# Strassen's algorithm for most of the input projection in an encoder-layer kernel

## The chip, the cores and the metric

The kernel runs on one core of a Trainium2 chip. The metric is the device time of one launch in microseconds (us): the median of three runs before the change is 1462.85 us (1462.04 to 1463.18). Engines are named as the profile names them: PE (matrix products; PEld is its weight load), DVE (vector), ACT (activation), POOL (GpSimd), SP (its queue issues the transfers, here called DMAs).

## The reference

One layer over 1024 tokens of width 1024. What the change touches is the first half:

```python
h = rmsnorm(x, g_mix_pre); proj = h @ w_in          # q, k, v of 8 + 8 heads of 64, and 8 forget gates
f_logit = proj[gates] + b_fgt; c = cumsum(log_sigmoid(f_logit))
y_fox = softmax(q k^T / 8 + c_t - c_s, causal) v    # 8 "f" heads
y_chk = softmax(q k^T / 8 + bias(t - s), band) v    # 8 "c" heads: own chunk of 64 + 8 before
y = concat(rmsnorm(y_fox), rmsnorm(y_chk)); x = x + rmsnorm(y @ w_out)
# then cross-attention into 256 memory tokens (mem), then a squared-ReLU MLP
```

## The kernel before

All products run in full float32 accuracy by splitting each operand in a high part (rounded to the engine's fp32r) and a low remainder, and doing three products (high-high, high-low, low-high): `mm3`, lines 193 to 195. A 128x128 block of weights times 512 tokens is therefore three PE instructions. 

Tokens are held transposed and split in `hT[th]`, th = 0, 1 for the two halves of 512 tokens. Heads come in eight pairs (`ORDER`, line 359: c0, c1, f0 to f3, c2, c3). A pair's queries are one block of 128 columns of `w_in`, its keys another, and for pairs 4 to 7 its values a third; the values of pairs 0 to 3 and the forget gates are made ahead. `project_steps` makes one such block: for each half of the tokens 8 blocks of contraction, so 2 x 8 x 3 = 48 PE instructions of 128x512. ACT and DVE take the result out of the accumulator in halves of 64 partitions (one head each): queries as scaled high and low parts stacked in one tile (`qs`), keys as a high tile `kd` and a low tile `kl`, each of which a DMA then copies to the other 64 partitions (line 849).

The order of everything is planned when the kernel is built. `Flow` is a list scheduler with guessed durations: streams of PE steps are generators (`value_steps`, `turn_steps`, `score_steps`, `side_steps`, `rstd_steps`, `filler_steps`), tried in that order, and whatever is ready first is issued; work of V (DVE), S (ACT), G (POOL) and D (the SP queue) is put in queues with levels. `Tokens` count free buffers (`u4`: tiles of 4 KB in each partition, 30 in all; `klo`, `sp`, `raw`, `w`, `mm` and so on). The chip then runs this fixed order on each engine, with semaphores for what the plan only guessed. The filler is the projection of all pairs and then the memory keys (`mk`) and values (`mv`); attention comes first wherever it can.

Attention of a head is a score product, a softmax (DVE, ACT, POOL), a transpose of the probabilities on the PE (line 711), their split (lines 717, 720) and the product with the values (line 754). The accumulator then holds four blocks, for the probabilities' high and low parts and the values' high and low parts on the two halves of the partitions. They are added in three steps: ACT copies one half of the partitions (771), DVE adds the other (766), POOL adds the high and low columns (768), and SP stores 64 rows in `od` (761).

The gates are turned to 8 rows of 1024 and put through eight vector operations there (`forget_gates`). The memory rows are normalised with their gain, stored in DRAM and loaded again (`mem_norm`, `mem_loads`).

Later parts of the kernel (the MLP and the first half of the memory output projection) already use Strassen's algorithm; the change does not touch them.

Of the kernel before, what the change touches and what calls it, by code (L numbers as in the profile page):

```python
# [22 lines left out]
P = 128  # L23
S = 1024
# [31 lines left out]
class Flow:  # L56
# [17 lines left out]

    def load(self, at, call, then=None, took=4.5, level=0):
        self.put("D", at, 0.55, call, then and (lambda end: then(end + took)), level)

    def chain(self, at, parts, then=None, level=2):

        if not parts:  # L80
            return then and then(at)
        eng, cost, call = parts[0]
        more = lambda end: self.chain(end + (2.5 if eng == "D" else 0.05), parts[1:], then, level)
        self.put(eng, at, cost, call, more, level)
# [21 lines left out]
    def run(self, streams, more=lambda: False):  # L106
        heads = [[g, next(g, None)] for g in streams]
        idle = 0
        while any(h[1] for h in heads) or more():
            for pump in self.pumps:  # L110
                pump()
            for h in heads:
                if h[1] and h[1][1]():
                    cost = h[1][0]
                    self.end = self.now + cost + 0.2
                    h[1] = next(h[0], None)
                    self.upto(self.now + cost)
                    idle = 0
                    break
            else:  # L120
                idle += 1
                assert idle < 4000, "no step can be taken"
                self.upto(self.now + 0.05)
# [12 lines left out]
def build(ctx, tc, nc, out, t):  # L136
# [106 lines left out]
    bfgt = const.tile([8, 1], F32, name="bfgt")  # L243
    gcol = const.tile([P, KC], F32, name="gcol")

    od = [[dr.tile([P, HT], F32, name=f"od{k}_{h}") for h in range(2)] for k in range(KC)]
    x1d = [dr.tile([P, D], F32, name=f"x1d{b}") for b in range(TB)]
    x2d = [dr.tile([P, D], F32, name=f"x2d{b}") for b in range(TB)]
    rd = dr.tile([8, 768], F32, name="rd")
    md = [dr.tile([P, D], F32, name=f"md{b}") for b in range(2)]  # L250
    cd = dr.tile([8, S], F32, name="cd")
    td = {k: [dr.tile([P, 2, HT], F32, name=f"{k}d{i}") for i in range(2)] for k in ("T1", "T2", "T3", "T4")}
# [23 lines left out]
    def bias_rows(part):  # L276

        if part == 0:
            rows.extend(p1.tile([8, 768], F32, tag="sp", bufs=5, name=k) for k in ("rrow", "rsrc"))
# [8 lines left out]
    fcol = p1.tile([P, TB, 8], F32, tag="o2", bufs=2, name="fcol")  # L288
# [52 lines left out]
    def value_leave(g, kb, ps):  # L341
# [12 lines left out]
        if g == 0:  # L354
# [9 lines left out]
                 q=4, mp=4, pt=1, xt=2, wq=0).items()}  # L364
    seen = {}

# [3 lines left out]
    def mark(key):  # L370
        return lambda at: seen.__setitem__(key, at)

# [12 lines left out]

    class Stock:
# [3 lines left out]
        def __init__(self):  # L390
            self.blocks = []
            for n, (kind, pr) in enumerate(ORDER):
                if n == 5:
                    self.blocks.append("norm")
                b = (0 if kind == "f" else 8) + pr
                self.blocks.append((("q", n), t["w_qk"][b], [P, KC, P]))
                if n > 3:
                    self.blocks.append((("v", n), t["w_v"][n - 4], [P, KC, P]))
                if n == 7:
                    self.blocks.append("mem")  # L400
                self.blocks.append((("k", n), t["w_qk"][b + 4], [P, KC, P]))
# [25 lines left out]
            self.raw, self.w, self.turned = {}, {}, 0  # L427
            self.to_load, self.to_split = list(self.blocks), []

        def load(self, n=1):  # L430
            for _ in range(n):
# [4 lines left out]
                self.to_split.append(key)  # L436
# [23 lines left out]
        def split_now(self, n):  # L460
# [6 lines left out]
            seen.update({("raw", key): 0.0 for key in self.to_split})  # L467
# [6 lines left out]
        def pump(self):  # L474

            while self.to_load:
                if isinstance(self.to_load[0], str):
                    n = 3 if self.to_load[0] == "norm" else 2
                    if not free["raw"].ready(n):
                        break  # L480
                    for _ in range(n):
                        free["raw"].take()
                    (mem_norm if self.to_load.pop(0) == "norm" else mem_loads)()
                    break
# [6 lines left out]
            while self.to_split and there(("raw", self.to_split[0])):  # L491
                key = self.to_split[0]
                home = self.home.get(key, "w")
# [19 lines left out]

    def forget_gates():

        z, e, l, u = [p1.tile([8, S], F32, tag="sp", bufs=5, name=f"f{n}") for n in "zelu"]
        parts = []
        for g in range(2):
            tr = mm_tile([8, 4, P], f"ftr{g}", "tr")
            for j in range(4):  # L520
                nc.tensor.transpose(tr[:, j, :], fcol[:, g * 4 + j, :], ident)
            parts.append(("V", 0.75, lambda g=g, tr=tr: nc.vector.tensor_scalar(
                z[:, g * HT:(g + 1) * HT], tr.rearrange("p a b -> p (a b)"), bfgt, None, op0=ALU.add)))

        parts += [
            ("V", 0.7, lambda: nc.vector.tensor_scalar(l, z, -1.0, None, op0=ALU.mult)),
            ("V", 1.2, lambda: nc.vector.tensor_tensor(l, l, z, op=ALU.min)),
            ("S", 1.1, lambda: nc.scalar.activation(e, l, AF.Exp)),
            ("V", 0.7, lambda: nc.vector.tensor_scalar(u, e, 1.0, None, op0=ALU.add)),
            ("S", 2.4, lambda: nc.scalar.activation(l, u, AF.Ln)),  # L530
            ("V", 1.3, lambda: nc.vector.scalar_tensor_tensor(e, u, 1.0, e, op0=ALU.subtract, op1=ALU.subtract)),
            ("S", 2.4, lambda: nc.scalar.activation(u, l, AF.Exp, scale=-1.0)),
            ("V", 1.2, lambda: nc.vector.tensor_tensor(e, e, u, op=ALU.mult)),
            ("V", 1.2, lambda: nc.vector.tensor_sub(e, e, l)),
            ("V", 1.3, lambda: nc.vector.scalar_tensor_tensor(e, z, 0.0, e, op0=ALU.min, op1=ALU.add)),
            ("V", 0.9, lambda: nc.vector.memset(u, 0.0)),
            ("V", 2.3, lambda: nc.vector.tensor_tensor_scan(l, e, u, 0.0, op0=ALU.add, op1=ALU.add)),
            ("D", 0.55, lambda: nc.sync.dma_start(cd, l))]

        def done(at):  # L540
            seen["gates"] = at
            for _ in range(4):
                free["sp"].give(at)

        for _ in range(2):
            free["tr"].take()
        flow.chain(flow.end, parts[:2], lambda at: [free["tr"].give(at) for _ in range(2)] and
                   flow.chain(at, parts[2:], done))
# [55 lines left out]
    def score_steps():  # L604
# [5 lines left out]
        for n, a in heads:  # L610
            kind, pr = ORDER[n]
            h = pr * 2 + a
            for g in groups(n):
                probs[n, a, g] = {}
                for q in (1, 0) if kind == "f" else (0, 1):
# [9 lines left out]
                    for j, (o, w) in enumerate(pieces):  # L625
# [3 lines left out]
                               lambda: there(("qk", n), ("bias", n, a)) and free["s"].ready()  # L629
# [96 lines left out]
    def value_steps():  # L726
        landed = [all_of(("od", k), 32) for k in range(2)]
        for n, a, g in units:
            kind, pr = ORDER[n]
            h = pr * 2 + a  # L730
            own, oth = HALVES[a]
# [25 lines left out]
            def leave(pv=pv, kind=kind, nm=f"{n}{a}{g}", own=own, oth=oth, kcol=kcol, g=g, step=1 if kind == "f" else -1):  # L757
                o2 = p1.tile([P, 2, 2, P], F32, tag="o2", bufs=2, name=f"o2{nm}")

                def store(end):  # L760
                    flow.load(end, lambda: nc.sync.dma_start(
                        od[kcol][g // 2][own, (g % 2) * 256:(g % 2) * 256 + 256],
                        o2[own, 0].rearrange("p a b -> p (a b)")), landed["fc".index(kind)], 2.2)

                def both(at):
                    flow.put("V", at, 0.7, lambda: nc.vector.tensor_add(  # L766
                        o2[own], pv[own, :, :, ::step], o2[own]), lambda end: (
                        free["pv"].give(end), flow.put("G", end, 0.8, lambda: nc.gpsimd.tensor_add(  # L768
                            o2[own, 0], o2[own, 0], o2[own, 1]), store)))

                flow.put("S", flow.end, 0.6, lambda: nc.scalar.activation(o2[own], pv[oth, :, :, ::step], AF.Copy), both)  # L771
# [20 lines left out]
    def project_steps(what, n, part):  # L792
# [6 lines left out]
        u = 3 if what == "v" else 2  # L799
        for th in range(2):  # L800
            cs = slice(th * HT, (th + 1) * HT)
            for kc in range(KC):
                yield (0.681, lambda: kc or there((what, n)) and free["mm"].ready() and
                       (th or free["u4"].ready(u) and (what != "k" or free["klo"].ready(2))))
                if kc == 0:
                    free["mm"].take()
                    if th == 0:
                        for _ in range(u):
                            free["u4"].take()
                        if what == "k":  # L810
                            for _ in range(2):
                                free["klo"].take()
# [3 lines left out]
            if what == "v":  # L816
                if th == 0:
                    vt[n] = u4(f"vt{n}", (P, S), F32)
                    vs2[n] = [u4(f"vs2_{n}{i}", (P, 4, 2, P)) for i in range(2)]
                flow.put("S", flow.end, 0.6, lambda th=th, ps=ps, cs=cs: nc.scalar.activation(vt[n][:, cs], ps, AF.Copy),  # L820
                         lambda at, th=th: (free["mm"].give(at), seen.__setitem__(("vt", n, th), at)), 1)
                continue
# [8 lines left out]
            for a, (own, oth) in enumerate(HALVES):  # L831
# [5 lines left out]
                if what == "q":  # L837
# [5 lines left out]
                    flow.put("S", flow.end, 0.6, hi, lambda at, lo=lo, last=last: flow.put(  # L843
                        "V", at, 0.7, lo, lambda end: (last(end), part(end)), 1), 1)
                else:
# [5 lines left out]
                    def then(at, lo=lo, last=last, copy=copy, d=d, l=l):  # L851
                        flow.load(at, lambda: copy(d), part, 2.3)
# [1614 lines left out]
```

## Time and profile before

| what | value |
|---|---|
| median of three runs | 1462.85 us |
| span of the profiled execution, first to last instruction | 1459.5 us |
| PE / DVE / ACT / POOL busy in it | 1447.7 / 996.0 / 820.7 / 421.0 us |
| instructions on PE | 7265 |
| bytes moved by DMA | 232.17 MB, 159 GB/s on average |
| first projection block (q of pair 0) starts | 56.8 us |
| last memory value product starts | 515.2 us |

The span is that of the one profiled execution; what lies between it and the launch's time is not in the profile. "Busy" of the PE counts overlapping instructions, so 99% says little of how dense its work is: the distance from one matmul's start to the next does. In the views by windows, the columns are the busy time of each engine with the number of instructions, the granted PE clock, the mean busy share of the 16 DMA engines, and GB/s.

### The profile page before, as it was taken

The page shows a single profiled execution, that of the slowest core. Times are in us where ns is not written, and L with a number is a line of the kernel's source. Part 1 is how long each engine was busy: PE and PEld are TensorE (multiplying, and loading weights), DVE is VectorE, ACT ScalarE, POOL GpSimd, SP SyncE. Part 2 cuts the span into 40 slices and gives each one's busy share as a digit, 9 for nine tenths or more (in the row PEclk, how much of TensorE's full clock was granted, in tenths as well). Part 3 has the DMA queues.
Part 4 walks back from the last instruction along what each step waited for, and adds up shares of the span by engine and source line. Part 5 has one row for each costly group of instructions (what it writes and reads, how often), then busy time and mean ns, then how long its engine had stood idle before and what let it go on. Part 6 is the DMA issues. An engine that isn't in the chain of part 4 may idle for free.

```text
span 1459.5 us, 21037 instructions
## 1 busy us (share of the span) xinstructions
PE 1447.7 (99%) x7265; PEld 1222.2 (84%) x7265; DVE 996.0 (68%) x1704; ACT 820.7 (56%) x1437; POOL 421.0 (29%) x520
## 2 busy tenths in 40 slices
PE   9999999999999999999999999999999999999998
PEld 8988888888889888888788888888888888888886
DVE  6777777767668847976873687765555666655576
ACT  6567677766677836555653465545555543444442
POOL 1245456555455301521332414343322000000021
PEclk9999999999999999999999999999999999999999
DMA  7132324321325584552541637754444785445565
GB/s 276 49 95 72 83 67 140 86 82 46 95 58 161 174 314 173 187 179 86 181 138 44 200 132 260 258 196 159 159 151 161 286 318 185 140 149 190 186 246 202
DMA packets 88987, 232.17 MB, mean 159 GB/s; under 512 B 10649, under 2 KB 14753, under 8 KB 88881
## 3 DMA queue, kind: packets, MB, share of 16 engines
q1 hardware_dynamic: 88736, 230.57, 47.6%
q8 instruction: 57, 0.93, 0.3%
q14 instruction: 50, 0.40, 0.1%
q10 hardware_dynamic: 144, 0.26, 0.1%
HBM read 167.30 MB, written 55.11 MB: 152 GB/s over the span
## 4 chain that ended last, share of the span: by engine, by line
PE 96%; DVE 2%; DMA 1%; ACT 1%; issue 0%; SPq 0%; DVEq 0%; ACTq 0%
PE pv L754 4%; PE fx L194 4%; PE fx L193 4%; PE fx L195 4%; PE ptr L711 4%; PE px L194 3%; PE fy L193 3%; PE px L195 3%; PE fy L195 3%; PE px L193 3%; PE fy L194 3%; PE mq L195 2%; PE q L193 2%; PE q L195 2%; PE q L194 2%; PE yw L193 2%
## 5 line engine op out<-in xcount | busy, mean ns | idle before, releaser
L717 DVE TENSOR_TENSOR phl<-ptr,phl 128x512 fp32r<-128x512 f32 (+1 forms) x152 | 92.5, 616 | 31.5 <-ACT phl L720 30.5
L2163 ACT ACTIVATE whif<-ra 128x1024 fp32r<-128x1024 f32 x37 | 39.2, 1061 | 130.3 <-PE fy L194 62.6
L2165 DVE TENSOR_TENSOR wlof<-ra,whif 128x1024 fp32r<-128x1024 f32 x37 | 45.3, 1225 | 91.7 <-ACT whif L2163 91.7
L720 ACT ACTIVATE phl<-ptr 128x512 fp32r<-128x512 f32 (+1 forms) x152 | 79.8, 540 | 40.3 <-PE ptr L711 38.5
L2285 POOL TENSOR_SCALAR rf<-sf 128x1 f32<-128x1 f32 x7 | 7.9, 1130 | 321.7 <-ACT jf L2266 321.4
L754 PE MATMUL pv<-phl,vs 128*128 128x512 f32 (+1 forms) x304 | 85.2, 366 | 0.2 <-DVE phl L717 0.2
L193 PE MATMUL fx<-vhif,whif 128*128 128x512 f32 x168 | 65.4, 389 | 0.0
L195 PE MATMUL fx<-vhif,wlof 128*128 128x512 f32 x168 | 65.4, 389 | 0.0
L194 PE MATMUL fx<-vlof,whif 128*128 128x512 f32 x168 | 65.4, 389 | 0.0
L754 PEld LDWEIGHTS pv<-phl,vs 128*128 128x128 f32 x304 | 55.2, 188 | 11.0 <-DVE phl L717 0.7
L2050 POOL TENSOR_TENSOR sc<-wf,wf 128x512 f32<-128x512 f32 x14 | 23.1, 1652 | 141.1 <-DMA wf<-in_w_ff 122.6
L768 POOL TENSOR_TENSOR o<-o 64x256 f32<-64x256 f32 x64 | 47.8, 747 | 53.1 <-DVE o L766 29.0
L193 PE MATMUL k<-hT_hi,whik 128*128 128x512 f32 x128 | 53.6, 419 | 0.0
L766 DVE TENSOR_TENSOR o<-pv,o 64x512 f32<-64x512 f32 x64 | 44.0, 688 | 13.5 <-ACT o L771 12.1
L193 PE MATMUL q<-hT_hi,whiq 128*128 128x512 f32 x128 | 51.6, 403 | 0.0
L193 PE MATMUL mq<-h2T_hi,whimq 128*128 128x512 f32 x128 | 51.4, 401 | 0.0
L195 PE MATMUL mq<-h2T_hi,wlomq 128*128 128x512 f32 x128 | 50.2, 392 | 0.2 <-DVE wlomq L455 0.2
L195 PE MATMUL k<-hT_hi,wlok 128*128 128x512 f32 x128 | 50.3, 393 | 0.0
L194 PE MATMUL k<-hT_lo,whik 128*128 128x512 f32 x128 | 50.3, 393 | 0.0
L195 PE MATMUL q<-hT_hi,wloq 128*128 128x512 f32 x128 | 50.2, 392 | 0.0
L194 PE MATMUL q<-hT_lo,whiq 128*128 128x512 f32 x128 | 50.2, 392 | 0.0
L194 PE MATMUL mq<-h2T_lo,whimq 128*128 128x512 f32 x128 | 50.1, 392 | 0.1
(696 smaller groups left out, 5014.5 us busy)
## 6 DMA issues: line engine op xcount, KB each, us to landing
ra<-gd SPq DMA_DIRECT2D x56, 512.0 KB, 3.8
wg<-in_w_ff SPq DMA_DIRECT2D x56, 512.0 KB, 5.6
wf<-in_w_ff SPq DMA_DIRECT2D x38, 512.0 KB, 3.9
gd<-s SPq DMA_DIRECT2D x48, 256.0 KB, 2.1
wrawmq<-in_w_mq SPq DMA_DIRECT2D x16, 512.0 KB, 4.3
gd<-u SPq DMA_DIRECT2D x32, 256.0 KB, 2.2
gd<-g SPq DMA_DIRECT2D x25, 256.0 KB, 2.2
wrawq<-in_w_qk SPq DMA_DIRECT2D x8, 512.0 KB, 4.4
```

What stands on the lines that cost most here:

```text
L193: nc.tensor.matmul(ps, lh, rh, start=start, stop=False, skip_group_check=more)
L194: nc.tensor.matmul(ps, lh, rl, start=False, stop=False, skip_group_check=more)
L195: nc.tensor.matmul(ps, ll, rh, start=False, stop=stop, skip_group_check=more)
L711: nc.tensor.transpose(tr[:, m, :], sp[:, k * P:(k + 1) * P], ident)
L717: flow.put("V", at, 0.7, lambda: nc.vector.tensor_sub(pl[:, live, :], tr[:, live, :], f(ph[:, live, :])), done)
L720: flow.put("S", flow.end, 0.6, lambda ph=ph, tr=tr, live=live: nc.scalar.activation(ph[:, live, :], tr[:, live, :], AF.Copy), split)
L754: nc.tensor.matmul(pv[:, :, qs_, :], v, hl[:, :, hs, :], start=c == 0 and turn == 0, stop=last)
L766: flow.put("V", at, 0.7, lambda: nc.vector.tensor_add(o2[own], pv[own, :, :, ::step], o2[own]), lambda end: (free["pv"].give(end), flow.pu ...
L768: free["pv"].give(end), flow.put("G", end, 0.8, lambda: nc.gpsimd.tensor_add(o2[own, 0], o2[own, 0], o2[own, 1]), store)))
L2050: eng.tensor_sub(sc[:, k1], r0[:, k0], r1[:, k0])
L2163: nc.scalar.activation(ah, ra, AF.Copy)
L2165: nc.vector.tensor_sub(al, ra, f(ah))
```

## The change

1. **Strassen for 16 of the 20 projection blocks.** Queries and keys of pairs 2 to 7 (six sets) and the values of pairs 4 and 5, 6 and 7 (two sets). A set takes two blocks of 128 columns as one, cut in 2 x 2 (two blocks by two halves of the contraction), against the tokens cut in 2 x 2. Seven products of 4 contraction blocks replace eight: 7 x 4 x 3 = 84 PE instructions for 96.
2. **Sums of tokens** (`TokenForms`): four forms T1 to T4 are made once of the normalised tokens, split and stored in DRAM (`qd`). Each set loads all of them again, 4 forms x 4 tiles of 512 KB (`Forms`).
3. **Sums of weights** (`Stock.unit`): four sums, and seven splits in four units of 128x1024, on ACT and on DVE or POOL, whichever the plan thinks free (`pick`).
4. **Sums of products** (`set_steps`): three products stay in the accumulator or are added to a copy. The result leaves with whole 128 partitions; DMAs then put the heads' halves and their copies in place, 3 for queries and 6 for keys of 64 partitions x 4 KB, some of them after one another.
5. **Pacing** (`run`, `share`): the filler goes first until it has 21.8 us + 1.1 times what the three attention streams have been given, instead of last.
6. **Value products leave whole**: ACT copies all of it, POOL adds high and low columns on 128 partitions, SP stores 128 rows in `oh`. The two halves are added later (`fold`): two loads, an addition, and a store in `od`, 16 times.
7. **Gates** keep the tokens in rows of partitions (128 x 8 x 8); only the cumulative sum runs on 8 rows. **Memory** rows are scaled without the round through DRAM, and the gain goes into their transposed split. The outputs of the first half of the tokens may start before the last score.

```diff
+    SETS = (("p", 2), ("p", 3), ("v", 4), ("p", 4), ("p", 5), ("v", 6), ("p", 6), ("p", 7))
+    SET_PRODUCTS = ((1, 0, "B11"), (1, 1, "T1"), (2, 0, "T2"), (2, 1, "B22"), (3, 0, "T3"), (3, 1, "B21"), (4, 0, "T4"))
-        for n in range(8):
-            part = all_of(("qk", n), 12)
-            yield from project_steps("q", n, part)
-            if n > 3:
-                yield from project_steps("v", n, part)
-            yield from project_steps("k", n, part)
+        ...
+        for i in range(len(SETS)):
+            yield from set_steps(i)
@@ set_steps
+        for p, (u, half, bn) in enumerate(SET_PRODUCTS):
+            for kc in range(4):
+                form = ("form", si, bn, kc)
+                yield 0.681, lambda: (bn[0] == "B" or there(form)) and (kc or there(("unit", st, u, half)) and room(p))
...
+                w = half * 4 + kc
+                mm3(ps, wh[:, w, :], wl[:, w, :], bh, bl, kc == 0 and p in (0, 1, 5), kc == 3, p != 5)
+                if bn[0] == "T":
+                    free[forms.bank[form[1:]]].give(flow.end)
@@ Forms
+            self.left = [(i, x, kc) for i in range(len(SETS)) for x in FORMS for kc in range(4)]
...
+                bank = "ring" if free["ring"].ready() else "u4"
+                if bank == "u4" and not (there("set 0") and free["u4"].ready(5) and len(self.tiles) < 8):
+                    break
...
+                    tl = self.tiles[key] = u4(f"{x}r{i}{kc}", (P, 2, HT))
+                    nc.sync.dma_start(f(tl), qd[x][kc // 2][:, kc % 2])
@@ set_steps, moves of a pair
+            def keys(x, at, then=None):
+                gone = all_of(("gone", n, then is None), 2, lambda end: move(
+                    end, lambda: x[n, 1][A], lambda: x[n, 1][B], then, 1))
+                move(at, lambda: x[n, 0][A], lambda: x[n, 1][A], gone, 0)
+                move(at, lambda: x[n, 0][B], lambda: x[n, 1][A], gone, 0)
+            def queries(at):
+                q, lo = (lambda a, c: qs[n, a][c]), (lambda c: tl["q"][c])
+                spent = all_of(("q lows", n), 2, free["klo"].give)
+                move(at, lambda: q(0, A), lambda: q(1, A), lambda end: move(
+                    end, lambda: q(1, A), lambda: lo(B), spent, 1), 0)
+                move(at, lambda: q(0, B), lambda: lo(A), spent, 0)
@@ value_steps, leave
-                    flow.put("V", at, 0.7, lambda: nc.vector.tensor_add(
-                        o2[own], pv[own, :, :, ::step], o2[own]), lambda end: (
-                        free["pv"].give(end), flow.put("G", end, 0.8, lambda: nc.gpsimd.tensor_add(
-                            o2[own, 0], o2[own, 0], o2[own, 1]), store)))
+                    free["pv"].give(at)
+                    flow.put("G", at, 0.8, lambda: nc.gpsimd.tensor_add(o2[:, 0], o2[:, 0], o2[:, 1]), store)
-                flow.put("S", flow.end, 0.6, lambda: nc.scalar.activation(o2[own], pv[oth, :, :, ::step], AF.Copy), both)
+                flow.put("S", flow.end, 0.6, lambda: nc.scalar.activation(o2, pv[:, :, :, ::step], AF.Copy), both)
@@ fold_one
+        for j, src in enumerate((oh[k][th].rearrange("(a p) n -> a p n", p=64)[::3], oh[k][th][64:192, :])):
+            flow.load(flow.now, lambda j=j, src=src: nc.sync.dma_start(x[:, j, :], src), both, 3.0, 1)
@@ Stock.unit
+            def sums(at, dst, op, x, y, key):
+                flow.pick(at, 0.7, 1.3, lambda v: getattr(adder(v), op)(dst, x, y), happens((key, st)), 2)
@@ attention_phase
-        flow.run([value_steps(), turn_steps(), score_steps(), side_steps(), rstd_steps(0),
-                  filler_steps(keep)])
+        flow.run([value_steps(), turn_steps(), score_steps(), side_steps(), rstd_steps(0, (0,)),
+                  filler_steps(keep)], share=lambda at: 21.8 + 1.1 * at)
```

507 lines of the change are left out of this document (392 added, 115 removed).

## The prediction

> **What bounds the kernel now.** I read the page first: busy times and the chain of work that ended last.
>
> ```profile
> span 1459.5 us, 21037 instructions
> PE 1447.7 (99%) x7265; PEld 1222.2 (84%) x7265; DVE 996.0 (68%) x1704; ACT 820.7 (56%) x1437; POOL 421.0 (29%) x520
> ...
> PE 96%; DVE 2%; DMA 1%; ACT 1%; issue 0%; SPq 0%; DVEq 0%; ACTq 0%
> ```
>
> The chain lies on PE for 96%. Since matmuls overlap, I then looked at distances between starts, in order of time, at the first query block, and at the stretch that the change rewrites, by windows (from the first scores to the last memory value product; the first rows after it serve below as prices).
>
> ```profile
> 56.82 0.39 PE L193 MATMUL q<-hT_hi,whiq 128*128 128x512 f32 x1
> 57.05 0.39 PE L194 MATMUL q<-hT_lo,whiq 128*128 128x512 f32 x1
> ...
> 59.34 0.39 PE L195 MATMUL q<-hT_hi,wloq 128*128 128x512 f32 x1
> ```
>
> ```profile
> 57.00:85.00 28.00, 28.00 (x129) 22.99 (x129) 18.49 (x22) 13.07 (x17) 9.85 (x11) 1.00 0.39 113
> 85.00:515.00 430.00, 429.26 (x2400) 367.63 (x2399) 320.14 (x835) 306.13 (x613) 216.42 (x314) 1.00 0.34 96
> 261.00:266.00 5.00, 5.00 (x29) 4.22 (x28) 3.37 (x7) 2.01 (x5) 0.74 (x2) 1.00 0.55 120
> 520.00:540.00 20.00, 20.00 (x90) 16.57 (x89) 6.58 (x9) 6.05 (x9) 0.00 (x0) 1.00 1.03 380
> 1160.00:1180.00 20.00, 20.00 (x90) 16.57 (x89) 13.83 (x14) 8.52 (x9) 0.00 (x0) 1.00 0.95 367
> 1180.00:1200.00 20.00, 20.00 (x90) 16.57 (x89) 13.03 (x11) 11.45 (x14) 0.00 (x0) 1.00 0.88 342
> ```
>
> Twelve matmuls of 128x512 start within 2.52 us: one each 0.229 us, though each lasts 0.39. In 85 to 515 PE is idle for 0.74 us of 430, at full clock. So here time is PE's number of instructions. DVE is busy for 74%, ACT 71%, POOL 50%, and the DMA engines for only a third: they have room, and it is they whom the change loads.
>
> **The change part by part.** *Products.* Eight sets save 96 - 84 = 12 instructions each: 96 x 0.229 = **22.0 us off PE**. Transposes, scores, value and memory products keep their number.
>
> *Forms.* 8 sets x 4 forms x 4 tiles = 128 loads of 512 KB on SP's queue, 67.1 MB that before were not there. The row of 1180 to 1200, nearly all loads of 512 KB with long rows, moves 342 GB/s at a share of 0.88: 389 GB/s when all engines are busy, so 524,288 bytes take 1.35 us of all 16, and 128 of them 172.5 us. Making the forms (8 sums, 8 splits, 16 stores, at 57 to about 90 us) falls in a stretch where DVE works 18.5 of 28 us, some 11 of them on the wide gate operations that leave; PE has four plain blocks to do there, 4 x 48 x 0.229 = 44 us. I price that at nothing; without the cover it would be the forms' chain, some ten operations of 1.2 us.
>
> *Moves.* The nearest rows are today's copies between partition halves, on SP's queue and in the list of DMA issues:
>
> ```profile
> 261.12 1.38 SPq L849 DMA_DIRECT2D kd<-kd  x2
> 262.56 0.58 SPq L849 DMA_DIRECT2D kl<-kl  x1
> 263.25 0.54 SPq L761 DMA_DIRECT2D od<-o  x1
> 263.88 0.55 SPq L849 DMA_DIRECT2D kl<-kl  x1
> ```
>
> ```profile
> ra<-gd SPq DMA_DIRECT2D x56, 512.0 KB, 3.8
> gd<-s SPq DMA_DIRECT2D x48, 256.0 KB, 2.1
> kd<-kd SPq DMA_DIRECT2D x32, 128.0 KB, 2.3
> od<-o SPq DMA_DIRECT2D x64, 64.0 KB, 1.9
> biasf<-cd SPq DMA_DIRECT2D x8, 512.0 KB, 4.5
> biasc<-rd SPq DMA_DIRECT2D x8, 320.0 KB, 3.6
> ```
>
> These four copies and one small store are what 261 to 266 moves: 120 GB/s at 0.55, that is 218 GB/s with all engines busy, against 389; and 128 KB land as late as 256 KB elsewhere. A pair's 9 moves of 262,144 bytes cost 9 x 1.20 = 10.8 us, six pairs 64.9. If among other transfers they run at 389 GB/s they cost 36.4. I take the former, since its row is the same kind of copy, and keep both.
>
> *Value products, biases, weights.* 64 stores of 131,072 bytes 21.6 us, 16 folds of 786,432 bytes 32.3, biases (8 x 512 + 8 x 320 KB) 17.5, all at 389 GB/s: 71.4 for all of attention. The sets' own weights: 16 x 1.35 = 21.6.
>
> *How long the sets last on PE.* 8 x 84 x 0.229 = 153.9 us; the pacing grants attention 1 us for 1.1 of filler, 139.9; transposes of values and gates some 3: **297 us**. Attention in all is the 430 less its filler. That is, from the list of groups by shape (80 to 520):
>
> ```profile
> L194 PE MATMUL k<-hT_lo,whik 128*128 128x512 f32 x112 | 44.0, 393 | 0.0
> ...
> L194 PE MATMUL q<-hT_lo,whiq 128*128 128x512 f32 x112 | 43.9, 392 | 0.0
> ...
> L194 PE MATMUL v<-hT_lo,whiv 128*128 128x512 f32 x64 | 25.2, 394 | 0.0
> ...
> L194 PE MATMUL mk<-mT_lo,whimk 128*128 128x256 f32 x64 | 18.1, 282 | 0.0
> ...
> L194 PE MATMUL mv<-wlomv,mT_hi 128*128 128x512 f32 x32 | 12.5, 390 | 0.0
> ```
>
> three times (112 + 112 + 64 + 32) x 0.229 and, at half of that, 3 x 64: 242 us, which leaves some 185 after side steps. Attention's share in the sets' stretch is 139.9 / 185 = 0.75.
>
> *The DMA engines in that stretch:* 172.5 + 21.6 + 64.9 + 0.75 x 71.4 = **312.6 us** of full work, or 284 with the cheap moves, against PE's 297. So two resources come out nearly equal; today it is a third against all. Filled without a gap the share reads 1.03 (520 to 540), which makes 312.6 / 1.03 = 303.5 us: 6.5 us over PE. With cheap moves nothing is over. The first form product follows 12 instructions (2.7 us) and as much attention after its load may start, and such loads land after 3.8 to 4.5: 0 to 1 us; I take 1. Stall: 7.5 us.
>
> [...]
>
> *DVE, ACT, POOL.*
>
> ```profile
> L766 DVE TENSOR_TENSOR o<-pv,o 64x512 f32<-64x512 f32 x64 | 44.0, 688 | 13.5 <-ACT o L771 12.1
> L841 DVE SCALAR_TENSOR_TENSOR qs<-q,qs 64x512 fp32r<-64x512 f32 x28 | 19.3, 689 | 8.3 <-ACT qs L840 7.7
> L848 DVE TENSOR_TENSOR kl<-k,kd 64x512 fp32r<-64x512 f32 x28 | 19.2, 687 | 9.9 <-ACT kd L847 9.6
> L455 DVE TENSOR_TENSOR wlomv<-wrawmv,whimv 128x1024 fp32r<-128x1024 f32 x8 | 10.3, 1284 | 0.3 <-ACT whimv L449 0.3
> L455 DVE TENSOR_TENSOR wlomk<-wrawmk,whimk 128x1024 fp32r<-128x1024 f32 x4 | 6.1, 1518 | 0.8 <-ACT whimk L449 0.8
> ```
>
> ```profile
> L458 POOL TENSOR_TENSOR wlok<-wrawk,whik 128x512 fp32r<-128x512 f32 x13 | 16.8, 1295 | 2.7 <-ACT whik L449 2.6
> ```
>
> DVE loses 44.0 and, six pairs x 8 x 0.688, 33. It gains 30 additions and lows of accumulators, and of 122 operations that either engine may do (7 splits and 4 sums a set, 3 lows a pair, 16 folds) say half: 91 x 0.69 = 63. That is 320 - 77 + 63 = 306 of about 408 us, 75% as before. POOL: 216 - 32 halves x 1.3 + 61 x 1.3 = 254, 62%. ACT: 16 splits of 1.06 and 48 head halves of 0.59 leave, 106 copies and splits of 0.6 come, 325 or so: 80%. None is the bound; price 0, as PE's work covers them, up to the rival below. The folds, the stores and the new moves stand in SP's one queue, where a transfer whose data are late holds all behind it:
>
> ```profile
> SPq L761 <- POOL o L768: 157.3, 46, 11.8
> ```
>
> Behind those waits now lie the form loads, and behind these PE; but the store comes one step (DVE's 0.69) sooner than today. Price 0; as a loss it is in the rival on the queue.
>
> **Sum.** 1459.5 - 22.0 + 7.5 = 1445.0 of span; the median lies 3.35 us above the profiled span (1462.85 against 1459.5): 1448.4, in round figures **1449 us**. By bounds of the moves, with the stall from 0 to 16.6 (no overlap above a share of 1, 312.6 - 297, and 1): 1441 to 1457.
>
> **The rivals.** *All hidden* (0.18): the moves cost 36.4 and slots for forms hold enough; PE stays dense and only the 22.0 us count: 1441. For it, 1160 to 1180: at 0.95 PE has no gap. Against it: that stretch has no moves between halves.
>
> *The DMA engines set the pace* (0.33), the other side: forms can be held only in a few slots (four, and more up to eight while five tiles are free), loads wait for a slot, and the one queue leaves gaps. If the share in the sets' stretch is that of 1160 to 1180, 0.95, it lasts 312.6 / 0.95 = 329 us, a stall of 32: 1459.5 - 22.0 + 32 + 3.35 = 1473. It decides as soon as the stretch is over 297 + 22 = 319 us, that is at a share under 0.98; at 0.92 it would be 1484. For it: two resources equally full seldom overlap well, and bursts come at the end of each set.
>
> *Late keys* (0.13): a pair's scores wait for moves in two hops, planned at 2.3 us each, which now queue behind form loads of 1.35 us each. Sets and attention run so close that pairs 4, 6 and 7 have no slack (by the pacing, at pair 6 attention has had 0.75 of its time and the filler is still short of the set). Two loads ahead of each hop, 2 x 2 x 1.35 = 5.4 us, at three pairs: 16 beside the 1 for the first form: 1458. For it: the plan knows nothing of a full queue. Against: a PE that waits lets the queue drain, so this does not add to the rival above.
>
> *Vector work late* (0.06): subtractions now alternate on DVE and POOL, and the row of wlomk, made while POOL works, is 18% above that of wlomv. 91 x 0.69 x 0.18 = 11 us if all of it reached PE: 1452.
>
> **Chances.** The forecast has 0.30; its own range is 1444 to 1457. About 0.2%, 2.9 us, is what a measurement here can tell from no change. Faster by more: all hidden 0.18, forecast 0.28, vector 0.05, half of late keys 0.06: 0.57. Within: 0.02 of the forecast, late keys 0.04, 0.02 of the DMA case: 0.08. Slower: 0.31 of the DMA case, the rest: 0.35. The range goes down to 1440 and up to 1480, which leaves out the far end of the DMA case.
>
> **What would show it.** PE at 96 instructions less; in the sets' stretch a DMA share near 1, against 0.34; idle time of PE, if any, released by form tiles (forecast), by scores waiting for moved keys (late keys), or spread over nearly all form products with a share of 0.9 to 0.95 (DMA case). If the share stays at 0.9 and PE has no gap, the price of the moves was too high. Wrong altogether if PE waits for DVE or POOL in the weight units, or if the plan itself leaves attention standing.

## The result and the profile after

The changed kernel takes **1600.4 us** (four runs, 1594.2 to 1602.2) beside 1462.5 (1462.0 to 1463.2) of the kernel before: a ratio of 1.0936, 95% interval 1.0919 to 1.0954. The forecast was 1449, the range ended at 1480, and the worst rival's far end was 1484. The page of the changed kernel, busy times and the chain that ended last:

```profile
span 1600.4 us, 21280 instructions
...
PE 1478.0 (92%) x7169; PEld 1235.3 (77%) x7169; DVE 997.7 (62%) x1688; ACT 830.9 (52%) x1485; POOL 482.8 (30%) x563
...
PE 74%; DMA 15%; DVE 4%; ACT 2%; SPq 2%; issue 2%; POOL 1%; DVEq 0%; POOLq 0%; ACTq 0%
```

The 96 instructions are gone (7169 for 7265), yet the chain is on PE for 74% of the span where it was 96%, and DMAs hold 15% of it. By windows: the start, the stretch of the eight sets, and what is left of attention (columns as above: busy time of PE, PEld, DVE, ACT, POOL, then granted clock, DMA share, GB/s).

```profile
60.00:125.00 65.00, 56.14 (x256) 45.41 (x255) 47.00 (x83) 35.82 (x65) 33.42 (x33) 0.92 0.64 218
125.90:566.00 440.10, 350.05 (x1690) 286.21 (x1689) 229.63 (x624) 233.34 (x498) 218.80 (x296) 0.88 0.78 251
566.00:652.00 86.00, 75.69 (x474) 68.32 (x472) 58.44 (x131) 58.17 (x112) 34.49 (x36) 0.94 0.66 199
```

The sets last 440 us and not 297. No resource is full there: PE is without work for 90 us, at a clock of 0.88; DVE, ACT and POOL are busy for half, and the DMA share is 0.78 where the forecast said near 1. So nothing ran out of capacity; work stood waiting. What it waited for is in the waits of the same stretch (total, times, longest). Those of PE are of several kinds, none of which has a third of the 90 us: DVE's pass over the scores, form tiles, moved keys, probabilities. Here are two of the longest, then those of POOL and DVE for folds, and two of SP (L849 is here the store of a product in `oh`, L1297 a fold's load):

```profile
PE stp7p L213 <- DMA T2r<-qT2d: 10.0, 2, 5.5
PE sf5g L727 <- DVE mnf4g L731: 9.3, 1, 9.3
```

```profile
POOL fold L1293 <- DMA fold<-oh: 59.5, 7, 12.3
...
DVE fold L1293 <- DMA fold<-oh: 34.1, 5, 11.7
```

```profile
SPq L849 <- POOL o L855: 51.6, 22, 7.5
...
SPq L1297 <- DMA oh<-o: 23.2, 6, 7.0
```

For 93.6 us in twelve pieces, POOL or DVE stand before a fold's addition whose loads have not landed. One such place, in the timeline (start, duration, line, and in brackets the idle time before it):

```profile
225.03 8.72 SPq L1297 DMA_DIRECT2D fold<-oh  x4
...
238.97 1.26 POOL L1293 TENSOR_TENSOR fold<-fold 128x512 f32<-128x512 f32 x1 [7.99 <-DMA fold<-oh]
240.18 0.29 POOL L689 TENSOR_SCALAR_AFFINE_SELECT biasf<-biasf 128x128 f32<-128x128 f32 x1
...
240.51 0.48 DVE L731 CUSTOM_DVE_ANT_0 spf1g<-sf1g,biasf,mnf1g 128x256 f32<-128x256 f32 x1 [7.04 <-POOL biasf L689]
...
241.06 0.58 PE L727 MATMUL sf1g<-k,q 128*128 128x256 f32 x1 [6.66 <-DVE mnf1g L731]
...
241.65 0.63 PE L213 MATMUL stv4p<-hT_hi,whiv4u 128*128 128x512 f32 x1
242.07 0.63 PE L214 MATMUL stv4p<-hT_lo,whiv4u 128*128 128x512 f32 x1
242.50 0.63 PE L215 MATMUL stv4p<-hT_hi,wlov4u 128*128 128x512 f32 x1
...
244.31 0.40 PE L213 MATMUL stv4p<-hT_hi,whiv4u 128*128 128x512 f32 x1
244.54 0.40 PE L214 MATMUL stv4p<-hT_lo,whiv4u 128*128 128x512 f32 x1
```

SP is at the four loads of two folds from 225.0 to 233.75 us. POOL stands 8 us before the addition; behind it in POOL's order is the mask of a bias (L689), behind that DVE's pass over the scores (L731), which adds the bias and frees their accumulator, and PE waits 6.7 us for one of these. Then the products start 0.42 to 0.43 us apart, and only from 244.3 on 0.23: the gap costs more than its length. The granted clock (third figure from the end) shows it, in 6 us without any product and in the 3 us behind the gap:

```profile
234.50:240.50 6.00, 0.00 (x0) 0.00 (x0) 0.00 (x0) 0.00 (x0) 1.51 (x2) 0.73 0.98 252
241.00:244.20 3.20, 3.14 (x9) 2.59 (x10) 2.16 (x7) 2.04 (x4) 0.00 (x0) 0.51 0.85 196
```

The experiments had two things to explain: why a fold's load of 256 KB takes so long, and what else there is beside the folds.

### The profile page after: what moved, and what is told of

It reads as the page before. It is cut to its first block, busy times and chain, and to the rows that moved or that the text cites. A ratio compares the mean times of both kernels' runs of the same rounds, so it can differ in the third digit from the quotient of the medians.

```text
span 1600.4 us, 21280 instructions
## 1 busy us (share of the span) xinstructions
PE 1478.0 (92%) x7169; PEld 1235.3 (77%) x7169; DVE 997.7 (62%) x1688; ACT 830.9 (52%) x1485; POOL 482.8 (30%) x563
## 4 chain that ended last, share of the span: by engine, by line
PE 74%; DMA 15%; DVE 4%; ACT 2%; SPq 2%; issue 2%; POOL 1%; DVEq 0%; POOLq 0%; ACTq 0%
DMA fold<-oh 5%; PE fx L214 4%; PE fx L213 4%; PE fx L215 4%; PE px L215 3%; PE fy L214 3%; PE px L213 3%; PE px L214 3%; PE fy L213 3%; PE fy L215 3%; PE ptr L800 2%; PE pv L842 2%; DMA kl<-kl 2%; DMA oh<-o 2%; PE mq L215 2%; PE mq L214 2%
## 5 line engine op out<-in xcount | busy, mean ns | idle before, releaser
L842 PE MATMUL pv<-phl,vs 128*128 128x512 f32 (+1 forms) x304 | 93.4, 392 | 12.7 <-DVE phl L806 12.6
L855 POOL TENSOR_TENSOR o<-o 128x256 f32<-128x256 f32 x64 | 50.3, 785 | 50.6 <-ACT o L857 43.1
L857 ACT ACTIVATE o<-pv 128x512 f32<-128x512 f32 x64 | 37.9, 591 | 32.9 <-PE pv L842 19.7
L213 PE MATMUL yw<-whiwo,yT_hi 128*128 128x512 f32 x128 | 51.1, 399 | 1.9 <-ACT yw L1505 1.9
L214 PE MATMUL yw<-wlowo,yT_hi 128*128 128x512 f32 x128 | 50.7, 396 | 0.0
L215 PE MATMUL yw<-whiwo,yT_lo 128*128 128x512 f32 x128 | 50.4, 394 | 0.0
L213 PE MATMUL fy<-vhif,whif 128*128 128x512 f32 x128 | 49.8, 389 | 0.0
L214 PE MATMUL fy<-vlof,whif 128*128 128x512 f32 x128 | 49.8, 389 | 0.0
L215 PE MATMUL fy<-vhif,wlof 128*128 128x512 f32 x128 | 49.8, 389 | 0.0
```

The source lines that it names most:

```text
L213: nc.tensor.matmul(ps, lh, rh, start=start, stop=False, skip_group_check=more)
L214: nc.tensor.matmul(ps, lh, rl, start=False, stop=False, skip_group_check=more)
L215: nc.tensor.matmul(ps, ll, rh, start=False, stop=stop, skip_group_check=more)
L842: nc.tensor.matmul(pv[:, :, qs_, :], v, hl[:, :, hs, :], start=c == 0 and turn == 0, stop=last)
L855: flow.put("G", at, 0.8, lambda: nc.gpsimd.tensor_add(o2[:, 0], o2[:, 0], o2[:, 1]), store)
```

## The experiments

Where no interval is given the time is that of one execution, beside the kernel before on the same chip (1461.2 to 1462.6). The two experiments with five executions span 1.9 and 2.8 us, the four of the changed kernel 8, so a single difference of a few us is weak evidence. At the start there were two theories: the folds (part 6) stand in the way, or the form loads (part 2) fill the queues.

### Folds or forms

Products leave as before, no folds:

```diff
-  o2 whole <- pv on ACT; POOL adds high and low on 128 partitions; store of 128 rows in oh; fold
+  o2[own] <- pv[oth] on ACT; DVE adds pv[own]; POOL adds on 64 partitions; store of 64 rows in od
```

> The changed kernel, but value products leave as before (half on ACT, half on DVE, 64 rows stored in od) and nothing is folded. Theory 'folds' (the fold's additions stand in the orders of POOL and DVE at a time planned from 3 us of load, while the load is held by the store it needs and by the form loads in the one queue; they account for 12% of the chain from 60 to 660 us, with the stores 18%, over 100 us): most of the loss goes, 1490 to 1530. Theory 'forms' (512 KB loads fill the queue and the DMA engines, whatever else is in it): only 42 us of DMA work of some 345 go and the loss shrinks by a fifth at most, 1565 to 1600.

Measured: **1517.3**. No loads of forms:

```diff
-                    x = forms.tiles.pop(form[1:])
-                    bh, bl = x[:, 0, :], x[:, 1, :]
+                    bh, bl = hT[1].hi(kc), hT[1].lo(kc)
```

> The changed kernel without the loads of token forms: the products with T1 to T4 read blocks of the plain tokens that are on the chip, so the output is not the layer's; PE's, ACT's, DVE's and POOL's instructions are as many as before. Theory 'forms': the queue is short again, transfers land in 2 to 4 us, PE is dense: 1440 to 1455. Theory 'folds': each fold load still stands behind the store it waits for, 2 us each instead of 3 to 12, and its addition still blocks POOL or DVE for some us: 1465 to 1500.

Measured: **1558.9**, between both theories. And both edits together:

> Both at once: old way out for the value products, and no loads of token forms (the T products read plain tokens; output not the layer's). It is the floor for PE with 96 instructions less: 1438 to 1450 by either theory. If it stays over 1460, the stalls come from the rest: moves of queries and keys in two hops, or the weight units' additions on DVE and POOL.

Measured: **1487.2**. The four corners: folds cost 83.1 us with form loads (1600.4 - 1517.3) and 71.7 without (1558.9 - 1487.2); form loads cost 41.5 with folds and 30.1 without. Each theory holds a part, folds the larger, and 46 us over the 1441 of "all hidden" belong to neither.

### What a fold costs, and why

The obvious suspect was its place: the load is planned at once, when its store is planned and has not landed, and the addition 3 us later. So it was planned later:

```diff
-        folds.append((k, th))                       # load at flow.now, addition 3.0 later
+        folds.append((k, th, at + 4.0))             # load when that time has come, addition 12.0 later
```

> The changed kernel, only the folds planned otherwise: their loads are issued no sooner than 4 us after the stores' planned landing (before: at once behind the store), and the addition is planned 12 us after that instead of 3. Same bytes, same instructions. Theory 'folds': the additions no longer block POOL and DVE, SP no longer stands on the store: 1500 to 1550. Theory 'forms': within 15 us of 1600.

Measured: **1573.3**: 27 us, a third at most. Then the fold was left out and only the leaving whole kept:

> The value products still leave whole (whole copy on ACT, addition on 128 partitions on POOL, store of 128 rows), but the two halves are never added: the loads, additions and stores of the 16 folds are left out, and the outputs read the first 128 rows as they are. If the folds' place in the fixed order is what costs (their loads stand in SP's queue behind the store that they wait for, their additions too early in the order of POOL or DVE), the time is that of the kernel that leaves its products as before, 1505 to 1530. If leaving whole costs (128 rows stored, wider addition on POOL, o2 held longer), it stays at 1570 or above.

Measured: **1508.7**, 8.6 us below the run whose products leave as before. Leaving whole costs nothing; a fold's loads, addition and store cost it all. All folds put off to the last set (`there("set 7")` as a further condition of the pump):

> All 16 folds are still done, but none before the last set of products has begun; until then nothing of them stands in any queue. If it is the place in the order, most of the 83 us come back: 1515 to 1545 (the folds themselves are 16 times about 2 us of transfers, some of it at the end). If it is the work or the bytes of the folds, 1575 to 1605.

Measured: **1604.3**, against the place. The loss had moved with the folds, as the windows of that run show: PE at work for 281 of 305 us up to 430 us, then for 64 of 140. In 430 to 590 us form tiles of the last set end five of PE's waits, 33.5 us.

```profile
125.00:430.00 305.00, 280.67 (x1454) 231.93 (x1453) 193.62 (x520) 197.31 (x420) 181.29 (x247) 0.95 0.87 288
440.00:580.00 140.00, 64.22 (x258) 51.12 (x258) 42.40 (x123) 43.80 (x96) 40.26 (x53) 0.71 0.63 196
```

And part 6 alone, in the kernel before, with no sets at all:

> The kernel before, with only part 6 of the change: value products leave whole and are folded later. Folds by themselves: with the 72 us that they cost where no form is loaded, 1500 to 1540. If they only hurt where Strassen's sets make the order tight (moves, paced filler), 1460 to 1480, since the plan of this kernel ends 2 us earlier than that of the kernel before.

Measured: **1539.9**, 78 us over the kernel before, with no form load under way. That made the trace easy to read. Here are 3 us in which only a fold's load is left, the two loads of a fold having been issued at 300.6 and 301.2 us:

```profile
305.00:308.00 3.00, 3.00 (x19) 2.42 (x18) 2.15 (x9) 1.68 (x3) 1.30 (x2) 1.00 0.13 49
```

A share of 0.13 is what 2 busy engines of 16 make, and 49 GB/s are moved, against 380 at a share of 1.03 from 520 to 540 us of before. The changed kernel has such stretches too: 0.13 and 51 GB/s from 231 to 234 us, in the timeline shown above. A fold has two loads of 256 KB. One reads rows 64 to 191 straight; the other reads rows 0 to 63 and 192 to 255 through a pattern of 2 x 64 x 512. At 49 GB/s 262,144 bytes take 5.3 us. What follows waits too: behind these loads, at 302.0, SP issues a store in `oh`, then stands for such a store until it issues the next fold's loads at 309.86, where the median store of this run lands in 1.7 us (the waits of 299 to 312 us):

```profile
SPq L1025 <- DMA oh<-o: 7.0, 1, 7.0
```

The slowest dimension of the second load's pattern is 2, as many as the engines that the share stands for; that the one sets the other was the author's guess. The test is to give that load 64 rows as its slowest dimension, in two loads for one, and leave all else:

```diff
-        for j, src in enumerate((oh[k][th].rearrange("(a p) n -> a p n", p=64)[::3], oh[k][th][64:192, :])):
+        for dst, src in ((x[0:64, 0, :], s[0:64, :]), (x[64:128, 0, :], s[192:256, :]), (x[:, 1, :], s[64:192, :])):
```

> The kernel before with part 6 alone, the narrow load again cut in two of 64 rows. Narrow load: the 78 us go, 1455 to 1470 (its plan ends 0.8 us before that of the kernel before). Place in the order: 1520 to 1540.

Measured, on the kernel before with part 6 alone: **1467.8** (ratio to the kernel before 1.0044, 1.0030 to 1.0058). Of 78 us, 72 are gone. The DMA issues (bytes each, median us from issue to landing), first with the narrow load, then without:

```profile
oh<-o SPq DMA_DIRECT2D x64, 128.0 KB, 1.7
fold<-oh SPq DMA_DIRECT2D x32, 256.0 KB, 9.1
```

```profile
oh<-o SPq DMA_DIRECT2D x64, 128.0 KB, 2.3
fold<-oh SPq DMA_DIRECT2D x32, 128.0 KB, 2.6
fold<-oh SPq DMA_DIRECT2D x16, 256.0 KB, 3.4
```

> The changed kernel, all 16 folds done at the same points; only the one load that reads rows 0 to 63 and 192 to 255 through a pattern whose slowest dimension is 2 becomes two loads of 64 rows. If the narrow load is what the folds cost (two of 16 DMA engines, about 49 GB/s, and everything behind it that needs those two engines), 1510 to 1535. If it is the place of the folds in SP's order and in that of POOL and DVE, 1575 to 1600, since no place changes.

Measured, on the changed kernel: **1551.7**. 48.7 of 83 us are the narrow load, and 34 are left. Whether these are the folds' place after all, or meetings with form loads:

> Folds with the narrow load cut in two, and no loads of token forms (the form products read plain tokens instead). Without forms the folds with the narrow load cost 72 us (1558.9 against 1487.2), with forms and without the narrow load 34 (1551.7 against 1517.3). If those 34 come from the folds' transfers meeting the form loads in full queues, 1485 to 1500 here; if from the folds' place in the order, about 1515 to 1525.

Measured: **1487.9**, 0.7 over the run with neither folds nor form loads. Without form loads, mended folds are free where they stand.

> The changed kernel with the narrow load cut in two, and the fold planned when its stores have landed (4 us after their planned landing) and its addition 7 us after the loads instead of 3. If the folds' remaining 34 us are their place in the order, 1520 to 1538 against 1551.7; if they are transfers in full queues, 1545 to 1560.

Measured: **1520.1**; with form loads, mended folds are nearly free if they are planned with the landing that they have. Both expectations hit, so it is both. Form loads make stores land late (4.3 us median in the run of 1551.7, 2.2 in that of 1487.9), and a load planned at once, and an addition planned 3 us on, then stand longer. SP's stand at the fold's load in the run of 1551.7, and below it in that of 1487.9:

```profile
SPq L1298 <- DMA oh<-o: 29.9, 10, 5.1
```

```profile
SPq L1295 <- DMA oh<-o: 12.8, 7, 4.9
```

POOL and DVE stand for the folds' loads for 34.5 us in the first and 19.7 in the second, where it cost no time that can be told. In the run of 1520.1 SP's stand is not among the longest waits.

### The forms' loads and their making

Half of the bytes, as many loads in the same places:

```diff
-                    nc.sync.dma_start(f(tl), qd[x][kc // 2][:, kc % 2])
+                    nc.sync.dma_start(f(tl[:, 0, :]), qd[x][kc // 2][:, kc % 2, 0])
```

> Products leave as before; of each form's tile only the high half is loaded (256 KB for 512; the low halves of the form products are taken from plain tokens). The 128 loads, their slots and their places in SP's queue stay. If the 30 us of the forms' loads are bytes (DMA share 0.84 in the sets' stretch), 1490 to 1503; if they are the waits in one queue for slots and loads, 1508 to 1518.

Measured: **1498.7**, 18.6 of the 30 us. So they are mostly bytes. The same 375 us in the runs without folds, with no form loads, half of them, and all:

```profile
125.00:500.00 375.00, 353.32 (x1937) 299.58 (x1937) 281.65 (x742) 270.61 (x566) 249.88 (x325) 0.97 0.40 105
```

```profile
125.00:500.00 375.00, 346.58 (x1844) 290.65 (x1843) 269.39 (x705) 258.57 (x539) 245.99 (x316) 0.96 0.67 190
```

```profile
125.00:500.00 375.00, 336.55 (x1744) 278.41 (x1742) 257.56 (x668) 246.92 (x514) 235.04 (x306) 0.96 0.84 268
```

PE does 1937, 1844 and 1744 instructions in the same time, at a DMA share of 0.40, 0.67 and 0.84. The cost comes long before a share of 1. What PE stands for in the last of these windows is mostly not the forms themselves: of 38 us, moved keys end eight waits with 16.0, form tiles two with 3.5. The longest of each kind:

```profile
PE sf4g L727 <- DMA k<-k: 3.4, 1, 3.4
...
PE stp3p L213 <- DMA T2r<-qT2d: 2.2, 1, 2.2
```

In the first of the windows, without form loads, moved keys still end 10.5 us of 22. Then the making of the forms was left out too:

> Products leave as before, no form is loaded (the form products take the plain tokens, as in the earlier run of this kind) and now none is made either: the 8 sums, 8 splits and 16 stores of the token forms are left out. If making them delays the start, where DVE is busy for 19.6 of 20 us, 1470 to 1477; if it is hidden under the four plain blocks, as predicted, 1484 to 1490, and the moves and the weight units are left.

Measured: **1472.2**. Making costs 15.0 us, with its 16 stores and the buffers that it holds. The start of the two runs, with the making and without:

```profile
57.00:125.00 68.00, 58.80 (x262) 47.47 (x261) 50.67 (x88) 35.79 (x65) 36.14 (x35) 0.92 0.59 195
```

```profile
57.00:125.00 68.00, 67.82 (x348) 56.88 (x347) 46.18 (x116) 41.20 (x85) 33.05 (x42) 1.00 0.32 88
```

With it PE issues 86 instructions fewer in 68 us: it is without work for 9.2 us, and its clock is 0.92, at most another 5 (0.08 x 68).

### The moves

> Products leave as before, all forms loaded; the moves of queries and keys are issued on ACT's queue instead of SP's. If the moves are late because they stand in SP's one queue behind form loads, biases and stores, 1485 to 1505; if the transfer itself or the vector work ahead of it sets their time, 1512 to 1530 (ACT then waits for them as well).

Measured: **1528.8**, 11.5 worse. The moves of keys land no sooner than from SP's queue (7.1 and 7.2 us median beside 6.7 and 6.8), so that queue was not what made them late; and ACT now stands for them (`ACT phl <- DMA kl<-kl` 6.7 us and `ACT qsum <- DMA k<-k` 6.8 us in its waits).

> The run without making and without loading forms (1472.2), with each of the 54 moves of queries and keys issued twice over. If the moves set part of what remains (1472 against 1441 with all hidden), 9 or more on top: 1481 to 1500. If they are hidden, 1470 to 1477, and what remains is the order itself (pacing and vector work that leave scores standing).

Measured: **1610.5**, 138.3 on top, far over both expectations. The second copy writes where the first one writes, so SP stands until the first has landed:

```profile
SPq L998 <- DMA k<-k: 47.4, 16, 4.9
SPq L998 <- DMA kl<-kl: 46.2, 16, 4.1
SPq L998 <- DMA q<-qsum: 30.0, 10, 3.1
...
SPq L998 <- DMA q<-q: 14.2, 6, 2.6
```

Together 137.8 us. The run does not price a hidden transfer, as it was meant to; it prices a queue that stands on one. About as much reached the time: eight of PE's waits there, of 7.6 to 13.5 us, are for moved keys, 84.0 us. (SP's long waits for `o` on POOL, 117 us in the run with single moves, did not.) In the change second hops stand like this too (7.5 and 9.5 us for `k` and `q` in SP's waits for L995), if they are planned before the first has landed, so the planned landing was raised from 2.3 to 4.0 us:

> As the run without making and without loading forms (1472.2), but the plan takes 4.0 us for a move's landing instead of 2.3, so that second hops and scores are planned when the first hop has really landed. If what remains of the loss is SP standing on second hops and scores standing on moves, 1456 to 1466; if it is attention that the pacing leaves without ready work, 1468 to 1478.

Measured: **1467.3**, 4.9 us, just over the better expectation. Without form loads this part is small.

### The rest, and all mends together

> All of the change but the sets and the folds: gates by token rows, memory rows without the round through DRAM, outputs of the first half earlier; projection in plain blocks, products leave as before, no pacing. If these parts are neutral, 1455 to 1466 (its plan ends 2 us before that of the kernel before); if part of the 55 us that remain without folds are theirs, above 1472.

Measured: **1467.3**, ratio 1.0043 (1.0029 to 1.0057): the other parts of the change cost 4 to 8 us by themselves.

> All of the change, with the three mends together: narrow load cut in two, folds planned when their stores have landed and 7 us for their loads, and 5.0 us for a move. Against 1520.1 without the last: 1500 to 1512 if the moves' planned landing matters as much under full queues, 1514 to 1526 if not. The bytes and the making of the forms stay, so it should not come under the kernel before.

Measured: **1522.9** beside 1520.1 without the later landing of moves. With form loads that mend brought nothing. No version came under the kernel before.

What is left in the run of 1467.3 with sets but without forms, by its windows, below the same windows of the kernel before:

```profile
125.00:380.00 255.00, 254.75 (x1377) 215.72 (x1376) 185.51 (x499) 178.27 (x360) 136.22 (x212) 1.00 0.29 83
380.00:460.00 80.00, 79.83 (x465) 69.23 (x464) 55.39 (x143) 53.71 (x109) 35.74 (x51) 1.00 0.40 108
```

```profile
125.00:380.00 255.00, 247.92 (x1320) 208.34 (x1320) 192.95 (x504) 182.93 (x380) 177.35 (x235) 0.99 0.35 92
380.00:460.00 80.00, 70.19 (x390) 60.03 (x389) 54.59 (x143) 53.19 (x114) 44.95 (x57) 0.94 0.53 139
```

PE is without work for 7.1 and 9.8 us, which is 16.5 more than before, and the clock in the last 80 us is 0.94. The waits of its PE are many and short, three of the longest for DVE's pass over the scores and for keys:

```profile
PE sf1g L727 <- DVE mnf1g L731: 3.8, 1, 3.8
PE sc4g L727 <- DVE mnc4g L731: 3.6, 1, 3.6
...
PE sc4g L728 <- DMA kl<-kl: 2.3, 1, 2.3
```

## Why the prediction was wrong

The account, each row one run against the one above it:

| from the changed kernel to the floor | time | difference |
|---|---|---|
| changed kernel | 1600.4 | |
| narrow load of the folds cut in two | 1551.7 | 48.7 |
| folds planned with their real landing | 1520.1 | 31.5 |
| products leave as before | 1517.3 | 2.8 |
| no loads of forms | 1487.2 | 30.1 |
| no making of forms | 1472.2 | 15.0 |
| moves planned with their landing | 1467.3 | 4.9 |
| predicted with all hidden | 1441 | 26 |

The differences hold in this order only: the form loads, for one, cost 41.5 with the folds in place and 30.1 without.

**The 22.0 us off PE**: the count was right, the 96 instructions are gone, and at full clock they still start 0.23 us apart. This step held, and it is the only gain that the runs show.

**The folds** are where the prediction failed, twice. It took "16 folds of 786,432 bytes 32.3" at 389 GB/s: a third of that, the narrow load, goes at 49. The pattern of that load stood in the quoted diff; its bytes were priced and its shape was not read. And it said of the folds, stores and moves in SP's one queue "Price 0", because "the store comes one step (DVE's 0.69) sooner". What matters is not when the store is planned but that a load which waits for it is issued straight behind it; measured, 83 us for both together. The prediction did say that in this queue "a transfer whose data are late holds all behind it", and then left the loss to the rival on the DMA engines and gave it no term of its own.

**The forms' loads**: a stall of 7.5 us was taken, 30.1 measured. The bytes were right (the runs show 268 GB/s with them, 105 without), but the sum let PE and the DMA engines overlap without loss up to a share of 1.03. The runs lose at 0.84, as transfers land late there. In the run of 1517.3, a form, the moves of the keys' low parts and a store of values (median us to landing last), where the rows of before had 1.9 to 4.5:

```profile
T1r<-qT1d SPq DMA_DIRECT2D x32, 512.0 KB, 7.8
...
kl<-kl SPq DMA_DIRECT2D x18, 256.0 KB, 6.8
...
od<-o SPq DMA_DIRECT2D x64, 64.0 KB, 4.0
```

The rival "The DMA engines set the pace" had the size of this part, 32 us, but by luck: its share of 0.95 was not reached over the sets (0.78 in the changed kernel, 0.84 in the run of 1517.3), and its sign, waits spread over nearly all form products, is not there (two waits, 3.5 us).

**Making the forms** was priced at nothing, under four plain blocks of 44 us. It costs 15.0. The prediction gave the price without that cover as some ten operations of 1.2 us, and that is near it. The cover was PE's; the delay is on DVE, whose order also holds the low parts of the first queries. A wait of PE in the changed kernel, in 57 to 125 us, shows it:

```profile
PE k L213 <- DVE qs L920: 5.1, 1, 5.1
```

**The moves**: price 64.9 us of DMA work, hidden; late keys 16 as a rival. The sign that the prediction gave for this rival is there: in the run of 1517.3 moved keys end 16.0 of the 38 us that PE stands between 125 and 500 us, more than anything else, beside 10.5 without form loads. The rival was set apart from the others and had 0.13; in the runs it comes beside them. What a mend of the moves would bring under form loads is open: later planning brought 4.9 without them and nothing with them.

**DVE, ACT, POOL**: none became the bound, as said; that they stand still for a late transfer in a fixed order was not asked. "Vector work late" hardly shows: in the changed kernel the weights' low parts end 1.6 of the 90 us of PE's waits in the sets.

**The rest**: 26 us over the floor remain, of which 4 to 8 belong to the gates, memory rows and outputs (the run without sets). Some 20 are idle PE and lower clock in the sets and just behind them. The prediction named this as what would make it "wrong altogether", that "the plan itself leaves attention standing", and gave it no chance. That it is the pacing is argued from the spread of short waits; no run took the pacing away.

A stall also cost more than its length (behind the gap of 6.66 us above, 3.2 us at a clock of 0.51), and no term of the sum had that. In the 440 us of the sets in the changed kernel, at a clock of 0.88, the lower clock cost by an estimate at most 53 us (0.12 x 440) beside the 90 of idle PE. It cost less than that, since the mean counts idle time as well: it is 0.73 in the 6 us above in which PE has no product.

## What to carry to other kernels

Price a transfer by the shape of its patterns, not by its bytes alone: look at its slowest dimension (2 here, at 49 GB/s; with that load cut in two of 64 rows, 72 of 78 us were gone), and in a trace at the DMA share while it runs alone (0.13 here). Where each engine follows a fixed order, a new operation costs whatever it makes the things behind it wait, so ask of each added load what it waits for, how long its landing takes under the load that the change itself adds, and what stands behind it in the queue and in the order of the engine that uses it. And when an experiment comes out between two theories, cross them (both, either, neither): here that showed at once that folds hurt even where no form is loaded.

## What the runs showed of the hardware

- A load through a pattern whose slowest dimension is 2 ran alone at a DMA share of 0.13, what 2 busy engines of 16 make, and 49 GB/s, and landed, in a group with as many straight loads of the same size, in 9.1 us in the median; cut in two of 64 rows, the parts landed in 2.6. Both are in the kernel before with part 6 alone.
- After the gap of 6.66 us shown above PE started products 0.42 to 0.43 us apart for about 3 us at a granted clock of 0.51, then 0.23.
- The addition of high and low columns takes POOL as long on 128 partitions as on 64, in the groups of the changed kernel and of the one whose products leave as before:

```profile
L855 POOL TENSOR_TENSOR o<-o 128x256 f32<-128x256 f32 x43 | 32.5, 757 | 33.2 <-ACT o L857 29.2 <-issue 4.0
```

```profile
L857 POOL TENSOR_TENSOR o<-o 64x256 f32<-64x256 f32 x53 | 40.6, 768 | 37.0 <-DVE o L855 23.0 <-issue 6.3 <-POOL biasf L689 2.5
```
